# A streaming encoder layer on one core: convolution tiles in their own memory pool, two more gate tiles as half-size products, eight convolution blocks moved to the attention's end

## The chip, the cores and the metric

The kernel runs on one core of a Trainium2 chip. The metric is device microseconds (us) of one execution. Three timed runs of the kernel before gave a median of 1925.06 us (1923.37 to 1925.43). One more execution was taken with the hardware profiler, and every time of an instruction below comes from that one.

## The reference

One layer of an encoder, for 1024 new frames of one stream and 32 frames of a running one (1056 columns in all), model width 1024:

```
h = rmsnorm(x) * (1 + sc1) + sh1            # scale and shift from the conditioning
q, k, v, g, a, cb, cc, ch, ga, gb = split(h @ w_in)
S, o = gated_linear_attention(q, k, v, log_sigmoid(a @ w_alpha + b) / 16, S0)
o    = rmsnorm_per_head(o) * silu(g)
y_a  = o @ w_gla_out
conv = causal_conv3(cc * ch) ;  y_b = (cb * conv) @ w_conv_out
x    = x + g1 * ((sigmoid(ga) * y_a + sigmoid(gb) * y_b) @ w_o)
x    = x + g2 * (silu(h2 @ w_gate) * (h2 @ w_up)) @ w_ffn_out     # h2 = second norm of x
```

All is float32. The kernel writes each fp32 product as three fp32r products, of a high and a low part of each operand (high by high, low by high, high by low).

## The kernel before, in words

Work runs in stages, each bounded mostly by TensorE (PE): projections for the attention up to about 285 us of the profiled execution; attention with the convolution branch, about 285 to 658 us; the gate tiles g, ga, gb (24 tiles of 128 output rows, eight each), about 658 to 924 us; then the output projections and the feed-forward part. Activations `h` lie in SBUF as eight tiles of 128 rows, each as a high and a low part (names `h_558`, `h_559` and so on).

*Attention and convolution.* The prompt is handled in four pairs of chunks of 128 frames (`prompt()`). A pair runs through seven levels of products with masks (PE writes `pslv`, VectorE copies it under a mask into the scores `s_sb`, and VectorE builds the next level's operand `tt`), then the diagonal (PE `psdg`, VectorE L832 into `s_sb`). Then for each chunk come the transposes of k (PE `pst`), the output (PE `pso`, which reads `s_sb`), its norm (PE `pms`) and the state update (PE `psn`, VectorE L589); the last thing is the normalized output `oT` (VectorE L620). The convolution `conv()` is a generator of 72 blocks, nine for each of eight tiles: three projections (cc, ch, cb) by three column blocks (384, 384 and 288 columns), 24 matmuls a block (helper `mm`, L135, output `ps`). Each `yield` of the attention lets the driver put such blocks into PE's program. The results of a block are taken out of PSUM by ScalarE (cc) or VectorE (ch by cc, L878; cb by the convolved row, L897); GpSimd starts the convolution (L885) and VectorE ends it with two long operations (L889). What blocks the attention has not used up follow it. The tiles `ccs`, `u` and `acc` of the convolution lie in the same pool as the attention's (`gl`, L537).

*The gate tiles.* A full-size tile is a projection in the same form as a conv projection: 3 blocks, 72 matmuls. The others go in pairs of tiles (`h_pair`) by a seven-product scheme of half-size matrices, which needs 168 matmuls of 264 columns for two tiles. Its operands are sums and differences of the quarters of `h` (`h_sums`, called for k = 0 to 3): for each k VectorE makes four sums (L965), GpSimd four differences (L971), ScalarE casts four high parts (L976) and VectorE subtracts four low parts (L977). The products are called B11 and B21, which read `h` itself, and T1 to T4, which need those sums; PE's line for them is L1055, output `psH`. Weight sums (L999) become a high part on ScalarE (L942) and a low part on VectorE or GpSimd (L943). Before, the first two tiles of gb (j = 0 and 4) are full-size, and `h_sums` runs beside them; the other 22 tiles go in eleven pairs.

The results of `h_sums` lie in pool `r2`, which takes the memory of `gl` after it closes. The order in which instructions stand on each engine is fixed when the program is built.

Of the kernel before, what the change touches and what calls it, by code (L numbers as in the profile page):

```python
# [7 lines left out]
F32 = mybir.dt.float32  # L8
# [5 lines left out]
P = 128  # L14
# [54 lines left out]
def hybrid_trunk(  # L69
# [464 lines left out]
    g2c = [mods[:, s, 40:48] for s in range(2)]  # L534


    with tc.tile_pool(name="gl", bufs=1) as gl:  # L537

        ones_r = gl.tile([P, P], F32R, name="ones_r")
        nc.vector.tensor_copy(ones_r, ones)  # L540
# [262 lines left out]
        def prompt():  # L803
            state = None
            npair = S // 256
            pair = load_pair(0)
            Tt = prep_level(pair, 0)
            for pr in range(npair):
                Z0, Z1, BB, vs = pair
                SS = s_sb[pr % SSETS]  # L810
                for li in range(len(LEVELS)):
                    nxt = prep_level(pair, li + 1) if li + 1 < len(LEVELS) else None
                    if li == DGL:
                        diag = [prep_diag(pair, ab) for ab in range(2)]
                    yield 1
                    if li in (0, 3):
                        yield 1
                    ps = psx.tile([P, 512], F32, tag="x", name=nm("pslv"))
                    for hd in range(H):
                        mm(ps[:, hd * P : (hd + 1) * P], Tt[:, 0, hd, :], Tt[:, 1, hd, :], True, True)  # L820
                    for ab in range(2):
                        nc.vector.copy_predicated(
                            SS[ab], mview(2 * li + ab, H), ps.rearrange("p (h n) -> p h n", h=H)
                        )
                    Tt = nxt
                chunk = [prep_chunk(pair, ab, pr > 0 or ab > 0) for ab in range(2)]
                yield 1
                for ab in range(2):
                    ps = psx.tile([P, 512], F32, tag="x", name=nm("psdg"))
                    mm(ps, ones_r, diag[ab][0], True, False)  # L830
                    mm(ps, ones_r, diag[ab][1], False, True)
                    nc.vector.copy_predicated(  # L832
                        SS[ab], mview(2 * len(LEVELS), H), ps.rearrange("p (h n) -> p h n", h=H)
                    )
                if pr + 1 < npair:
                    pair = load_pair(pr + 1)
                for ab in range(2):
                    qs, ks, dec = chunk[ab]
                    yield 1
                    yield 1  # L840
                    kt, vsp = transpose_k(ks), split_v(vs[ab])
                    psos, sq = out_chunk(vs[ab], SS[ab], qs, state)
                    if ab == 1 and pr + 1 < npair:
                        Tt = prep_level(pair, 0)
                    yield 1
                    finish_chunk(psos, sq, 256 * pr + ab * P)
                    state = state_update(state, dec, kt, vsp)
            nc.scalar.dma_start(sp_out.rearrange("h p v -> p h v"), state)
# [17 lines left out]

        def conv():
            for j in range(KT):
                ccs = gt([P, T], "ccs", 2)
                u = gt([P, UE], "u", 2)  # L870
                acc = gt([P, T + 2], "acc", 1)

                def ev_cc(b, ps, ccs=ccs):
                    nc.scalar.copy(ccs[:, blk(b)], ps)

                def ev_ch(b, ps, ccs=ccs, u=u):
                    for lo, hi, nat in csegs(b):
                        nc.vector.tensor_tensor(nat(u, 2), ps[:, lo - BO[b] : hi - BO[b]], ccs[:, lo:hi], op=ALU.mult)  # L878

                nc.gpsimd.memset(u[:, 0:2], 0.0)  # L880
                nc.sync.dma_start(u[:, S + 2 : S + 4], cache[j])
                yield from gemm_steps(load_w(w_in[CC0 + j]), h, ev_cc)
                yield from gemm_steps(load_w(w_in[CH0 + j]), h, ev_ch)
                n = T + 2
                nc.gpsimd.tensor_scalar(  # L885
                    acc[:, :n], u[:, 0:n], convp[:, 0, j : j + 1], convp[:, 3, j : j + 1], op0=ALU.mult, op1=ALU.add
                )
                for i in (1, 2):
                    nc.vector.scalar_tensor_tensor(  # L889
                        acc[:, :n], u[:, i : i + n], convp[:, i, j : j + 1], acc[:, :n], op0=ALU.mult, op1=ALU.add  # L890
                    )
                nc.gpsimd.tensor_copy(cco[:, 0, j, :], u[:, S : S + 2])
                nc.gpsimd.tensor_copy(cco[:, 1, j, :], u[:, UE - 2 : UE])

                def ev_cb(b, ps, acc=acc, j=j, ccs=ccs):
                    for lo, hi, nat in csegs(b):
                        nc.vector.tensor_tensor(ccs[:, lo:hi], ps[:, lo - BO[b] : hi - BO[b]], nat(acc, 0), op=ALU.mult)  # L897
                    if b == NB - 1:
                        nc.scalar.dma_start(c_d[j], ccs[:, :T])

                yield from gemm_steps(load_w(w_in[CB0 + j]), h, ev_cb)
# [15 lines left out]
        nc.scalar.dma_start(cc_out, cco.rearrange("p s j r -> p (s j r)"))  # L917


    r2 = ctx.enter_context(tc.tile_pool(name="r2", bufs=1))  # L920

    t4 = ctx.enter_context(tc.tile_pool(name="t4", bufs=1, reuse_waits="tile"))

# [6 lines left out]
    def unit(tag, shape, dt=F32R):  # L930
        if tag == "r1":
            return r1.tile(shape, dt, tag="r1", name=nm("u"))
        return r2.tile(shape, dt, tag=tag, name=nm("u"), bufs={"a": 12, "x": 8}[tag])

    gran = [0]

    def granule(src, lo_eng):
# [4 lines left out]
        nc.scalar.copy(hi, src)  # L942
        lo_eng.tensor_tensor(lo, src, f(hi), op=ALU.subtract)  # L943
        return hi, lo

    def gate_block(j, b, ps):
        sb = td()[:, : wd(b)]
        nc.scalar.activation(sb, ps[:, : wd(b)], AF.Sigmoid)  # L948
        nc.scalar.dma_start(sb_d[j][:, blk(b)], sb)

# [6 lines left out]
    def h_sums(k):  # L959
        raw = []  # L960
        for kk in (k, k + 4):
            hi, lo = h[kk]
            for e in range(2):
                t = td().rearrange("p (q n) -> p q n", q=2)
                nc.vector.tensor_tensor(t, f(quarters(hi)[e]), f(quarters(lo)[e]), op=ALU.add)  # L965
                raw.append(t)
        b11, b12, b21, b22 = raw

        def sub(x, y):
            t = td().rearrange("p (q n) -> p q n", q=2)  # L970
            nc.gpsimd.tensor_tensor(t, x, y, op=ALU.subtract)  # L971
            return t

        def keep(i, t):
            u = unit("x" if i == T4 else "a", [P, 2, 2, CW])
            nc.scalar.copy(u[:, 0], t)  # L976
            nc.vector.tensor_tensor(u[:, 1], t, f(u[:, 0]), op=ALU.subtract)  # L977
            hsum[i][k] = u

        t1 = sub(b12, b11)  # L980
        keep(T1, t1)
        t2 = sub(b22, t1)
        keep(T2, t2)
        keep(T3, sub(b22, b12))
        keep(T4, sub(b21, t2))
# [111 lines left out]

        return done


    ws = [load_w(w_in[GB0 + j]) for j in (0, 4)]
    for n, (j, w) in enumerate(zip((0, 4), ws)):
        h_sums(2 * n)
        h_sums(2 * n + 1)
        gemm(w, h, lambda b, ps, j=j: gate_block(j, b, ps))
    for j in range(4):
        h_pair(G0, j, AF.Silu, done_g)
    for j in range(4):
        h_pair(GA0, j, AF.Sigmoid, done_to(sa_d))
    for j in range(1, 4):  # L1110
        h_pair(GB0, j, AF.Sigmoid, done_to(sb_d))

    some_done(99)
# [16 lines left out]
    for j in range(KT):  # L1130
        w = load_w(w_gla_out[j])
        if j < 2:
            pool, tag = ((psm, "m"), (psx, "x"))[j]
            ps = [pool.tile([P, 512], F32, tag=tag, name=nm("ps"))[:, : wd(b)] for b in range(NB)]
            for k in range(KT):
                for b in range(NB):
                    ah, al = og[k]
                    mm(ps[b], w[0][:, k, :], ah[:, blk(b)], k == 0, False)
                    mm(ps[b], w[0][:, k, :], al[:, blk(b)], False, False)
                    mm(ps[b], w[1][:, k, :], ah[:, blk(b)], False, k == KT - 1)  # L1140
            for b in range(NB):
                attn_block(j, b, ps[b])
        else:
            gemm(w, og, lambda b, ps, j=j: attn_block(j, b, ps))
        pr = tuple(unit("a" if j < 4 else "x", [P, T]) for _ in range(2))
        for q in range(2):
            craw = td()
            nc.sync.dma_start(craw, c_d[j][:, cols(q)])
            split(craw, pr[0][:, cols(q)], pr[1][:, cols(q)], "act", "pool")
        cpair.append(pr)  # L1150
# [71 lines left out]
    def make_ops(q):  # L1222
        n = 0
        for i in (B11, B21, T2, T3, T1, B22, T4):
            ops[q][i] = []
            for _ in range(2):
# [1 line left out]
                if q == 0 and n < 12:  # L1228
                    t = r2.tile(sh, F32R, tag="a", name=nm("op"), bufs=12)
                elif q == 0 or n < 6:  # L1230
                    t = r2.tile(sh, F32R, tag="x", name=nm("op"), bufs=8)
                else:
                    t = r1.tile(sh, F32R, tag="r1", name=nm("op"))
                ops[q][i].append(t)
# [314 lines left out]
    x1 = [None] * KT  # L1549

    def load_x1(j):
        x1[j] = r2.tile([P, T], F32, tag="x", name=nm("x1"), bufs=8)
        load(x1[j], x1_d[j])

    turns = [(p, j) for p in range(len(PARTS)) for j in range(4)]
# [265 lines left out]
```

## Time and profile before

| | |
|---|---|
| median of three timed runs | 1925.06 us |
| the profiled execution, its own time | 1930.39 us |
| its span | 1928.6 us |
| PE busy | 1834.0 us (95%) |
| VectorE (DVE) busy | 1382.9 us (72%) |
| ScalarE (ACT) busy | 790.1 us (41%) |
| GpSimd (POOL) busy | 797.7 us (41%) |
| mean granted clock of PE | 0.978 |

A row of instructions gives a line of the code, an engine, an operation, the tile written and the tiles read; where an engine sat idle, what it waited for follows an arrow. Clock 1.00 is TensorE's upper level.

### The profile page before, as it was taken

Reading aid. Unit: us, or ns where it says so; the run is one execution under the profiler, and the core shown is the slowest. Engines: PE = TensorE matmul, PEld = TensorE weight load, DVE = VectorE, ACT = ScalarE, POOL = GpSimd, SP = SyncE. Lnnn points to the kernel's source line nnn. Section 1 sums busy time; section 2 is a strip of 40 time slices with the busy share of each in tenths; the row PEclk is TensorE's granted clock in tenths of the full one; section 3 lists DMA queues with packets and bytes.
Section 4 is the critical chain, followed back from the end, with each engine's and each line's share of the span. In section 5 each row is a group of like instructions: output and inputs, shape, how many; then the busy total and the mean of one; then the engine's idle time right before and its main releaser. Section 6 shows DMA issues by size and latency. Waiting matters only on the chain. (4 is left out here: it accounts for less than half of the span.)

```text
span 1928.6 us, 35501 instructions
## 1 busy us (share of the span) xinstructions
PE 1834.0 (95%) x13517; PEld 1809.4 (94%) x13517; DVE 1382.9 (72%) x2543; ACT 790.1 (41%) x1641; POOL 797.7 (41%) x649
## 2 busy tenths in 40 slices
PE   6799889999999979999999999899999999999997
PEld 5698888999999979999999999899999999999997
DVE  7999967775866777543114478789888888678865
ACT  5434344444342355544212256435444444222243
POOL 6753437574754452112442243122223222255474
PEclk9799999999999989999999999999999999999998
DMA  7587644323221226335854454213433434686522
GB/s 276 179 286 230 210 167 129 99 89 94 88 77 56 87 88 231 134 110 195 308 178 135 127 175 151 78 61 128 172 131 129 171 126 151 212 299 235 213 95 90
DMA packets 166269, 298.45 MB, mean 155 GB/s; under 512 B 20593, under 2 KB 81905, under 8 KB 166098
## 3 DMA queue, kind: packets, MB, share of 16 engines
q1 hardware_dynamic: 117170, 211.90, 33.6%
q10 hardware_dynamic: 48928, 84.27, 11.8%
q8 instruction: 106, 1.74, 0.4%
q14 instruction: 65, 0.53, 0.1%
HBM read 211.78 MB, written 84.33 MB: 154 GB/s over the span
## 5 line engine op out<-in xcount | busy, mean ns | idle before, releaser
L135 PE MATMUL ps<-h,whi 128*128 128x384 f32 (+2 forms) x1440 | 347.3, 326 | 6.9 <-DVE vst L518 4.8
L143 POOL TENSOR_TENSOR wlo<-raw,whi 128x512 fp32r<-128x512 f32 (+2 forms) x160 | 218.1, 1382 | 298.9 <-ACT whi L139 212.9
L1330 PE MATMUL psX<-op,wg 128*128 128x264 f32 (+1 forms) x2112 | 273.2, 286 | 6.3 <-DVE bz L1361 3.9
L1330 PEld LDWEIGHTS psX<-op,wg 128*128 128x128 f32 x2112 | 264.2, 189 | 9.1 <-DVE bz L1361 5.9
L135 PEld LDWEIGHTS ps<-h,whi 128*128 128x128 f32 x1440 | 251.8, 190 | 8.2 <-issue 5.2
L943 POOL TENSOR_TENSOR wg<-raw,wg 128x512 fp32r<-128x512 f32 x66 | 96.9, 1468 | 367.0 <-ACT wg L942 304.3
L135 PE MATMUL ps<-h,wlo 128*128 128x384 f32 (+2 forms) x720 | 233.6, 325 | 0.0
L135 PE MATMUL ps<-u,whi 128*128 128x264 f32 (+2 forms) x1064 | 226.2, 306 | 2.1 <-ACT whi L139 1.9
L135 PEld LDWEIGHTS ps<-u,whi 128*128 128x128 f32 x1064 | 176.3, 189 | 3.0 <-ACT whi L139 2.1
L135 PE MATMUL ps<-u,wlo 128*128 128x264 f32 (+2 forms) x532 | 162.8, 306 | 0.0
L224 DVE CUSTOM_DVE_ANT_0 junk<-wm,cb 128x1024 f32<-128x1024 f32 x96 | 153.7, 1601 | 4.9 <-DMA wm<-in_w_modT 3.4
L1330 PE MATMUL psV<-op,wg 128*128 128x264 f32 (+1 forms) x1056 | 137.9, 286 | 1.1 <-ACT wg L942 1.1
L135 PEld LDWEIGHTS ps<-h,wlo 128*128 128x128 f32 x720 | 136.8, 190 | 0.2 <-issue 0.2
L1055 PE MATMUL psH<-u,wg 128*128 128x264 f32 x1056 | 133.6, 286 | 3.2 <-ACT wg L942 3.2
L1055 PEld LDWEIGHTS psH<-u,wg 128*128 128x128 f32 x1056 | 131.1, 190 | 3.7 <-ACT wg L942 3.7
L1330 PEld LDWEIGHTS psV<-op,wg 128*128 128x128 f32 x1056 | 133.2, 189 | 1.3 <-ACT wg L942 1.3
L139 ACT CAST whi<-raw 128x512 fp32r<-128x512 f32 (+2 forms) x164 | 87.7, 579 | 103.5 <-PE ps L135 58.6
L942 ACT CAST wg<-d 128x512 fp32r<-128x512 f32 x132 | 81.6, 622 | 109.4 <-PE psV L1330 36.0
L943 DVE TENSOR_TENSOR wg<-d,wg 128x512 fp32r<-128x512 f32 x121 | 92.7, 768 | 44.2 <-ACT wg L942 43.9
L1055 PE MATMUL psH<-h,wg 128*128 128x264 f32 x792 | 101.9, 287 | 5.9 <-ACT d L948 5.9
L1611 PE MATMUL psX<-u,wg 128*128 128x264 f32 x768 | 106.2, 284 | 0.0
L1055 PEld LDWEIGHTS psH<-h,wg 128*128 128x128 f32 x792 | 99.3, 190 | 6.1 <-ACT d L948 6.1
(321 smaller groups left out, 4019.5 us busy)
## 6 DMA issues: line engine op xcount, KB each, us to landing
wm<-in_w_modT SPq DMA_DIRECT2D x64, 512.0 KB, 4.5
raw<-in_w_in SPq DMA_DIRECT2D x124, 256.0 KB, 3.2
op_d<-st ACTq DMA_DIRECT2D x56, 528.0 KB, 5.1
u<-op_d SPq DMA_DIRECT2D x56, 528.0 KB, 6.1
raw<-in_w_ffn_in SPq DMA_DIRECT2D x88, 256.0 KB, 3.2
u<-og_d SPq DMA_DIRECT2D x16, 528.0 KB, 8.4
raw<-in_w_o SPq DMA_DIRECT2D x32, 256.0 KB, 3.1
raw<-in_w_ffn_out SPq DMA_DIRECT2D x32, 256.0 KB, 5.1
```

Of the source, the lines that this page charges most:

```text
L135: nc.tensor.matmul(ps, lhsT, rhs, start=start, stop=stop)
L139: nc.scalar.copy(hi, raw)
L143: nc.gpsimd.tensor_tensor(lo, raw, f(hi), op=ALU.subtract)
L224: nc.vector.tensor_tensor_reduce(junk, wm, cb[:, st, :], 1.0, 0.0, ALU.mult, ALU.add, mods[:, st, j : j + 1])
L942: nc.scalar.copy(hi, src)
L943: lo_eng.tensor_tensor(lo, src, f(hi), op=ALU.subtract)
L1055: nc.tensor.matmul(bank[i][q], wt[l][:, k, :], h_operand(i, k, q, r), start=i in (B11, B21, T3) and k == 0 and n == 0, stop=k == 3 and n == 2,
L1330: nc.tensor.matmul(ps, l[:, k, :], r[:, k, :], start=first and k == 0 and i == 0, stop=k == 3 and i == 2, skip_group_check=True,)
L1611: nc.tensor.matmul(ps, w[l][:, k, :], o[k][:, r, c], start=first and k == 0 and i == 0, stop=k == n - 1 and i == 2, skip_group_check=True,)
```

## The change

1. A new pool `cv` is opened before `gl` and holds `ccs`, `u` and `acc` of the convolution. The pool `r2` is split: `r2x` (tag "x", five buffers) lies where `cv` was, `r2` (tags "a", twelve, and "y", three) where `gl` was, and both wait for the tiles whose memory they take, one by one, not for the whole pool. With this the `h_sums` need no longer follow the convolution's end.
2. One of two `yield 1` between the diagonal and the transposes of a chunk goes, eight in all.
3. The two full-size gate tiles go: gb's j = 0 and 4 become a twelfth pair, and the four `h_sums` stand ahead of all pairs.

```diff
-    with tc.tile_pool(name="gl", bufs=1) as gl:
+    with tc.tile_pool(name="cv", bufs=1) as cv, tc.tile_pool(name="gl", bufs=1) as gl:
...
                     qs, ks, dec = chunk[ab]
                     yield 1
-                    yield 1
                     kt, vsp = transpose_k(ks), split_v(vs[ab])
...
-                ccs = gt([P, T], "ccs", 2)
-                u = gt([P, UE], "u", 2)
-                acc = gt([P, T + 2], "acc", 1)
+                ccs = cv.tile([P, T], F32, tag="ccs", name=nm("ccs"), bufs=2)
+                u = cv.tile([P, UE], F32, tag="u", name=nm("u"), bufs=2)
+                acc = cv.tile([P, T + 2], F32, tag="acc", name=nm("acc"), bufs=1)
...
-    r2 = ctx.enter_context(tc.tile_pool(name="r2", bufs=1))
+    r2x = ctx.enter_context(tc.tile_pool(name="r2x", bufs=1, reuse_waits="tile"))
+    r2 = ctx.enter_context(tc.tile_pool(name="r2", bufs=1, reuse_waits="tile"))
...
-    ws = [load_w(w_in[GB0 + j]) for j in (0, 4)]
-    for n, (j, w) in enumerate(zip((0, 4), ws)):
-        h_sums(2 * n)
-        h_sums(2 * n + 1)
-        gemm(w, h, lambda b, ps, j=j: gate_block(j, b, ps))
+    for k in range(4):
+        h_sums(k)
     for j in range(4):
         h_pair(G0, j, AF.Silu, done_g)
     for j in range(4):
         h_pair(GA0, j, AF.Sigmoid, done_to(sa_d))
-    for j in range(1, 4):
+    for j in range(4):
         h_pair(GB0, j, AF.Sigmoid, done_to(sb_d))
```

The rest of the diff gives later users of the old eight "x" buffers one of "x" or "y" each.

On PE the program is the same up to the last row of the block after `psdg` of pair 0. There, before, a second block of 24 matmuls stood ahead of the transposes:

```order
L135 MATMUL ps_3491<-h_608,wlo_3380 128x288
L135 MATMUL ps_3534<-h_558,whi_3524 128x384
...
L135 MATMUL ps_3534<-h_608,wlo_3525 128x384
L560 MATMUL pst_3562<-ident,kk_3425 128x128 x4
L135 MATMUL pso_3575<-s_sb_2735,v_3009 128x128 x4
L135 MATMUL pso_3580<-s_sb_2735,v_3009 128x128 x4
```

Now the transposes stand right behind the first block, and two matmuls of the next block ahead of `pso`:

```order
L135 MATMUL ps_3494<-h_608,wlo_3383 128x288
L560 MATMUL pst_3522<-ident,kk_3428 128x128 x4
L135 MATMUL ps_3569<-h_558,whi_3559 128x384
L135 MATMUL ps_3569<-h_559,whi_3559 128x384
L135 MATMUL pso_3535<-s_sb_2738,v_3012 128x128 x4
L135 MATMUL pso_3540<-s_sb_2738,v_3012 128x128 x4
```

So 24 conv matmuls left this place; in each of the four pairs there are now 24 between `psdg` and the first transposes, and were 48. Within the first three steps between levels the conv matmuls of pair 1 go from 24, 24, 48 to 27, 13, 38, of pair 2 from 21, 18, 48 to 7, 28, 36 (its last four steps from 24 each to 8, 22, 21 and 22, and 17 instead of 4 ahead of its first level), of pair 3 from 26, 19, 48 to 24, 27, 23.

The second place is PE behind the attention. Before, the last norm product `pms` was followed by the rest of three conv blocks (70 conv matmuls), three blocks of the first full-size gate tile (from `ps_6507`), one of the second, and then the first half-size products:

```order
L135 MATMUL pms_6246<-nrm_6214,ones_r 128x512
...
L135 MATMUL ps_6507<-h_558,whi_6431 128x384
...
L135 MATMUL ps_6647<-h_558,whi_6441 128x384
...
L1055 MATMUL psH_6743<-h_588,wg_6776 128x264
```

Now the same `pms` is followed by the last three projections of the convolution (first rows `ps_6138`, `ps_6226`, `ps_6325`) and then by half-size products at once:

```order
L135 MATMUL pms_5990<-nrm_5958,ones_r 128x512
...
L135 MATMUL ps_6138<-h_558,whi_6128 128x384
...
L135 MATMUL ps_6226<-h_558,whi_6216 128x384
...
L135 MATMUL ps_6325<-h_558,whi_6315 128x384
...
L1052 MATMUL psH_6558<-h_558,wg_6566 128x264
L1052 MATMUL psH_6559<-h_558,wg_6566 128x264
```

Behind `pms` there are now 242 conv matmuls, 172 more than before, and no full-size gate tile. The products B11 and B21 (48 matmuls) stand before T3 and T2 in both programs. The second PSUM bank of B11 (`psH_6559`) is the one that conv block `ps_6325` leaves.

The third place is VectorE at the attention's end. Before, the last convolution results (L897) and a weight's low part stood between the last `oT` and the first sums:

```order
L620 SCALAR_TENSOR_TENSOR oT_6245<-pso_6199,glag,nrm_6250 128x4x128
L897 TENSOR_TENSOR ccs_5973<-ps_6350,acc_5975 128x128 x3
L897 TENSOR_TENSOR ccs_5973<-ps_6378,acc_5975 128x128 x2
L897 TENSOR_TENSOR ccs_5973<-ps_6378,acc_5975 128x32
L943 TENSOR_TENSOR wg_6747<-raw_6731,wg_6747 128x512
L965 TENSOR_TENSOR d_6451<-h_558,h_559 128x528
L965 TENSOR_TENSOR d_6453<-h_558,h_559 128x528
```

Now the sums (L962, which was L965) follow `oT` directly, and the last conv tile's operations stand among them:

```order
L620 SCALAR_TENSOR_TENSOR oT_5989<-pso_5943,glag,nrm_5994 128x4x128
L962 TENSOR_TENSOR d_6438<-h_558,h_559 128x528
...
L945 TENSOR_TENSOR wg_6566<-raw_6550,wg_6566 128x512
...
L877 TENSOR_TENSOR u_6124<-ps_6226,ccs_6123 128x128 x3
...
L888 SCALAR_TENSOR_TENSOR acc_6125<-u_6124,convp,acc_6125 128x1058
...
L896 TENSOR_TENSOR ccs_6123<-ps_6325,acc_6125 128x128 x3
...
L945 TENSOR_TENSOR wg_6630<-d_6628,wg_6630 128x512
```

Among the 32 rows of the sums there are now nine small rows of L877, nine of L896, two long ones of L888 and one L945; GpSimd has its conv operation (L884) and one weight part among its sixteen differences. The low part of T2's first weights (`wg_6630`) stands at the end of the sums in both programs.

## Rows read from the trace of the kernel before

**Rows 1.** The page: busy time, share of the span and instructions.

```profile
PE 1834.0 (95%) x13517; PEld 1809.4 (94%) x13517; DVE 1382.9 (72%) x2543; ACT 790.1 (41%) x1641; POOL 797.7 (41%) x649
```

**Rows 2.** Stretches (us): length, busy by engine (instructions), granted clock, DMA share, GB/s.

```profile
657.82:669.38 11.56, 11.56 (x74) 11.56 (x73) 9.54 (x11) 3.21 (x6) 7.91 (x5) 1.00 0.54 172
720.00:900.00 180.00, 180.00 (x1484) 180.00 (x1483) 100.09 (x168) 91.67 (x204) 40.07 (x28) 1.00 0.46 154
645.80:657.82 12.02, 12.02 (x77) 11.97 (x77) 10.46 (x19) 3.60 (x4) 3.37 (x5) 1.00 0.28 92
657.82:702.36 44.54, 33.34 (x199) 32.40 (x197) 40.62 (x43) 17.70 (x32) 28.06 (x18) 0.88 0.22 72
690.00:695.00 5.00, 0.00 (x0) 0.00 (x0) 4.87 (x6) 1.37 (x3) 3.65 (x3) 0.66 0.00 0
396.50:652.00 255.50, 247.66 (x1644) 244.35 (x1643) 179.08 (x285) 99.89 (x178) 145.72 (x117) 0.99 0.25 78
```

**Rows 3.** Waits of PE, 655 to 710: waiting for, us in total, times, longest.

```profile
PE psH L1055 <- ACT d L948: 5.9, 1, 5.9
PE psH L1055 <- ACT wg L942: 3.2, 2, 2.4
PE ps L135 <- ACT d L948: 2.1, 1, 2.1
```

**Rows 4.** Timeline of VectorE: start us, duration us, instruction, idle before.

```profile
655.20 1.41 DVE L620 SCALAR_TENSOR_TENSOR oT<-pso,glag,nrm 128x512 f32<-128x512 f32 x2
660.41 1.93 DVE L965 TENSOR_TENSOR d<-h,h 128x528 f32<-128x528 f32 x3
698.79 0.69 DVE L977 TENSOR_TENSOR u<-d,u 128x528 fp32r<-128x528 f32 x1
701.89 1.28 DVE L943 TENSOR_TENSOR wg<-d,wg 128x512 fp32r<-128x512 f32 x2
```

**Rows 5.** Groups by line, 660.3 to 699.6: busy us, mean ns, idle before.

```profile
L971 POOL TENSOR_TENSOR d<-d,d 128x528 f32<-128x528 f32 x16 | 26.3, 1662 | 11.5 <-DVE d L965 8.3 <-DMA sb_d<-d 3.1
L977 DVE TENSOR_TENSOR u<-d,u 128x528 fp32r<-128x528 f32 x16 | 22.5, 1415 | 1.9 <-ACT u L976 1.3
L965 DVE TENSOR_TENSOR d<-h,h 128x528 f32<-128x528 f32 x16 | 13.7, 898 | 1.3 <-POOL d L971 1.2
```

**Rows 6.** Timeline of VectorE, operations of the convolution.

```profile
656.53 0.68 DVE L897 TENSOR_TENSOR ccs<-ps,acc 128x128 f32<-128x128 f32 x3
647.83 2.46 DVE L889 SCALAR_TENSOR_TENSOR acc<-u,convp,acc 128x1058 f32<-128x1058 f32 x1 [0.88 <-POOL acc L885]
650.81 1.31 DVE L889 SCALAR_TENSOR_TENSOR acc<-u,convp,acc 128x1058 f32<-128x1058 f32 x1
```

**Rows 7.** Timeline of PE: first output products of each pair, and the last norm product.

```profile
363.36 0.39 PE L135 MATMUL pso<-s_sb,v 128*128 128x128 f32 x2
447.24 0.39 PE L135 MATMUL pso<-s_sb,v 128*128 128x128 f32 x2
531.55 0.39 PE L135 MATMUL pso<-s_sb,v 128*128 128x128 f32 x2
615.39 0.28 PE L135 MATMUL pso<-s_sb,v 128*128 128x128 f32 x1
645.80 0.40 PE L135 MATMUL pms<-nrm,ones_r 128*128 128x512 f32 x1
```

**Rows 8.** Timeline of VectorE: the diagonals into the scores, pairs 0 to 3; then pair 1's last level.

```profile
361.16 1.36 DVE L832 COPY_PREDICATED s_sb<-masks,psdg 128x512 f32<-128x512 uint8 x2
441.21 1.35 DVE L832 COPY_PREDICATED s_sb<-masks,psdg 128x512 f32<-128x512 uint8 x2
526.63 1.36 DVE L832 COPY_PREDICATED s_sb<-masks,psdg 128x512 f32<-128x512 uint8 x2
607.45 1.35 DVE L832 COPY_PREDICATED s_sb<-masks,psdg 128x512 f32<-128x512 uint8 x2
435.06 0.75 DVE L751 TENSOR_TENSOR tt<-tt,z 128x512 f32<-128x512 f32 x1 [2.62 <-DMA z<-q_d]
```

More of the change, by code (lines that the diff above doesn't have):

```diff
@@ L932, in unit @@
             return r1.tile(shape, dt, tag="r1", name=nm("u"))
-        return r2.tile(shape, dt, tag=tag, name=nm("u"), bufs={"a": 12, "x": 8}[tag])
+        if tag in ("x", "y"):
+            return (r2x if tag == "x" else r2).tile(shape, dt, tag=tag, name=nm("u"), bufs={"x": 5, "y": 3}[tag])
+        return r2.tile(shape, dt, tag=tag, name=nm("u"), bufs=12)
     gran = [0]
@@ L944, in granule @@
         return hi, lo
[L946 to L949, printed above, removed]
     B11, B21, B22, T4, T1, T2, T3 = range(7)
@@ L974, in keep @@
         def keep(i, t):
-            u = unit("x" if i == T4 else "a", [P, 2, 2, CW])
+            u = unit("a" if i != T4 else "y" if k < 3 else "x", [P, 2, 2, CW])
             nc.scalar.copy(u[:, 0], t)
@@ L1144, in hybrid_trunk @@
             gemm(w, og, lambda b, ps, j=j: attn_block(j, b, ps))
-        pr = tuple(unit("a" if j < 4 else "x", [P, T]) for _ in range(2))
+        pr = tuple(unit("a" if j < 4 else "y" if 2 * j + r > 12 else "x", [P, T]) for r in range(2))
         for q in range(2):
@@ L1230, in make_ops @@
                 elif q == 0 or n < 6:
-                    t = r2.tile(sh, F32R, tag="x", name=nm("op"), bufs=8)
+                    t = unit("y" if n in (0, 1, 2) else "x", sh)
                 else:
@@ L1551, in load_x1 @@
     def load_x1(j):
-        x1[j] = r2.tile([P, T], F32, tag="x", name=nm("x1"), bufs=8)
+        x1[j] = unit("y" if j < 3 else "x", [P, T], F32)
         load(x1[j], x1_d[j])
```

## The prediction

> **What bounds the kernel now.** I read the page's busy shares first: PE is busy 95% of the span, VectorE 72% [rows 1]. So PE's program is the length of the kernel, except where PE stands still or runs at the low clock. Then the stretches around the change, one after the other. In 720 to 900 us PE has no gap at the granted clock 1.00 and does 1484 half-size matmuls in 180.00 us, 0.1213 us each [rows 2]: here only the number of matmuls counts. In the attention, 396.5 to 652, PE is busy 247.66 of 255.50 us and VectorE 179.08, 70% [rows 2]: PE leads, because conv blocks fill its waits. Between them, from 657.82 to 702.36, PE is busy 33.34 of 44.54 us at a mean clock of 0.88 [rows 2]. That is the one soft place. The waits of PE there add up to 11.2 us: 5.9 and 2.1 behind ScalarE, 3.2 for a weight's high part [rows 3]. In 690 to 695 PE does nothing, and VectorE is busy 4.87 of 5 us [rows 2]. So VectorE's sums set this place, and from 660.41, their start, to 702.36, when the low part of T2's first weight exists (701.89, two operations of 1.28 us in all), 41.95 us pass [rows 4].
>
> **Part 1, two gate tiles.** A full-size tile takes 11.56 us at clock 1.00 [rows 2]; two are 23.12 us. The twelfth pair takes 168 half-size matmuls at 0.1213 us, 20.38 us. Difference: -2.74 us, sure, as both run where PE leads. The weights of a pair cost ScalarE and VectorE more than those of two full tiles, but VectorE is busy 100.09 and ScalarE 91.67 of the 180 us [rows 2], and PE never waits there, so this is hidden.
>
> **Part 2, the hand-over.** Measure it from the last `pms` (645.80 [rows 7]) to the start of T2. Before that is 56.56 us (702.36 less 645.80). PE's work in it: 12.02 us of attention and conv [rows 2], 23.12 us of full tiles, 48 products of B11 and B21 at 0.1213, 5.82; in all 40.96. Lost: 15.6 us, of which 11.2 are waits and the rest low clock.
>
> Now PE's work there is 12.02 us, plus 172 conv matmuls, plus the same 5.82. A conv matmul costs the 72nd part of a tile, so 172 are 27.6 us: 45.44 in all. VectorE sets the length again, if the sums do not become quicker. They start directly behind `oT`, whose end is 656.61 (655.20 and 1.41), 10.81 us behind `pms`; before it was 14.61. Then they take 41.95 us, and what the last conv tile puts among them. Eighteen small operations in six groups of three at 0.68 us are 4.1 us; two long ones lie between 1.31 and 2.46 us each, so 2.6 to 4.9 [rows 6]; one weight part is 0.64 (half of the two at 701.89 [rows 4]) or, beside GpSimd, some twice that. That is 7.3 to 10.3 us on VectorE. It has under 4 us of idle in the sums [rows 5], which can swallow some. GpSimd gets a conv operation and a weight part too, and each of its differences already holds up VectorE. Bounds: 5 us (idle swallowed) and 11; I take 8, near the sum of the rows with a little swallowed. T2 then starts 10.81 + 41.95 + 8 = 60.8 us behind `pms`, and 60.8 less 45.4 gives 15.3 us lost: -0.3 us against before, with bounds of -3.3 and +2.7.
>
> PE cannot use this time with something else. B11's second bank is left by conv block `ps_6325`, which VectorE takes out late in the sums, some twelve operations before T2's weight; PE is in order, so T3 and T2 stand behind it. The conv tail moved here fills PE, but PE had full-size tiles here before: one cover replaces the other.
>
> Why the sums are slow matters here. L977 alone took 0.69 us (at 698.79, after GpSimd's last difference [rows 4]); beside GpSimd's differences its mean was 1415 ns [rows 5]. The Trainium skill, "SBUF — State Buffer", section "Who interferes with whom", says that a VectorE instruction with two SBUF inputs contends with a GpSimd instruction that reads SBUF, and that one with at most one SBUF input does not. The rows agree with the first half. By the second half the eighteen small conv operations, which read one input from PSUM, would leave GpSimd free to run, and then only the two long ones and the conv operation on GpSimd would lengthen the sums, about 5 us; the sum by that reading is the lower bound of this part.
>
> **Part 3, the attention's cover.** The same 172 matmuls, 27.6 us, leave the attention. Where PE is the bound there, this time is gone from it, and part 2 has counted it at the other end. What comes back as waiting is the cost. The place is `pso`, which needs `s_sb` with the diagonal. 24 conv matmuls ahead of it are 4.2 us (two blocks of a tile are 384 columns and one is 288; 24 of 384 take 4.2 of the 11.56 us).
>
> - Pair 0: `pso` came at 363.36 [rows 7], would come at 359.5 (4.2 less, two conv matmuls put ahead); the scores are complete at 362.52 (361.16 and 1.36 [rows 8]), the first chunk's at about 361.8. Wait 2.3 to 3.0, I take 2.7.
> - Pair 1: 447.24 less 4.2 is 443.0, scores at 442.56: no wait from this alone. But 18 conv matmuls (2.9 us at 11.56/72 each) also left the steps between the first levels, while VectorE's chain waits 2.62 us for a load at 435.06 [rows 8] and will not come earlier for it. Wait 0 to 2.5, I take 2.2.
> - Pair 2: 531.55 less 4.2 is 527.35, scores at 527.99: 0.6. Between its levels 39 are fewer (6.3 us), against 13 more ahead of the first (2.1 us); if nothing of VectorE's chain moves up, 6.9, and with the 13 as cover 4.8. I take 2.0, nearer to the place's own 0.6, as VectorE's idle 30% [rows 2] lets part of its chain move up.
> - Pair 3: 615.39 less 4.2 is 611.2, scores at 608.80: room of 2.4; 19 fewer between levels (3.1 us) leave 0 to 0.7. I take 0.5.
>
> Together 7.4 us, with bounds of 0 (pair 0 waits, and other waits shrink by as much) and 13.1, or more if the levels themselves begin to wait. VectorE has one conv tile less to do in the attention, which helps it; that is why I do not add to the sum for the levels.
>
> **Part 4, the rest.** The new pool, the buffer tags and the later loads change which tile waits for which. The stages behind run without PE waits of size, and the order there is nearly the same; 0.
>
> **The sum.** -2.7, -0.3 and +7.4 give +4.4 us. The profiled execution took 1930.39 us, so it would take 1934.8. The median is 5.3 us lower, so the forecast on its scale is 1929.5 us.
>
> **The rivals.**
>
> A. Faster: the attention has slack. VectorE is idle 30% of it and gets less to do, so behind pair 0 its chain moves up with PE, and what pair 0 waits comes back from waits between levels that shrink; and the sums take only 5 us more (the reading of part 2). Then -2.7, -3.3 and 0: -6.0, 1919 us. For it: VectorE's 70%. Against it: its idle time there is waiting for loads and for PE's own levels, as at 435.06, which a shorter PE program does not move up. It would be still less if the sums hid wholly behind the conv tail, but 41.95 us of sums do not fit beside the 28.8 us of it that are left behind `oT` (12.02 and 27.6 less 10.81).
>
> B. No change: the waits in the attention are about 3 us, hand-over as forecast: 1925 us. This differs from the forecast only in the size of part 3.
>
> C. Much slower: sums and conv lock each other, and the levels wait too. VectorE and GpSimd run almost in turn in the sums; if every conv operation also delays a GpSimd difference on which a later L977 waits, part 2 becomes +2.7, and if the six steps between levels that lost ten conv matmuls or more wait 1 us more each, part 3 becomes 7.4 and 6 and, with pair 2 at 4.8, 16.2: 1941 us. It decides from the point where VectorE's chain between levels is longer than the conv left there, as with the 7 matmuls (1.1 us) in pair 2.
>
> D. The change does not do what it says: the sums still wait for the attention's memory. A unit may not be written before the tiles under it are free, and `oT` is among them until it is stored. For it: the sums are the first users of that memory. Against it: VectorE's first sums are not in that pool. If so the sums start as late as before, 3.8 us later than I reckon: +8.2, 1933 us.
>
> **Chances.** Forecast (slower by 2 to 7 us) 0.40, A 0.27, B 0.18, C 0.07, D 0.08. A measurement of this kernel can tell about 0.2%, 3.85 us, from no change. Faster by more than that is most of A: 0.23. Slower by more is the upper half of the forecast, C and D: 0.42. Within: 0.35. The range must hold A and reaches towards C: 1918 to 1937. The forecast's own is 1927 to 1932.
>
> **What would show it.** Right: a wait of PE for L832 of 2 to 3 us before `pso` in pair 0 and shorter ones in pairs 1 and 2; a gap of PE of over 10 us after the last conv block, ended by the eviction of `ps_6325` or by VectorE; T2 about 61 us behind the last `pms`; 0.1213 us for a half-size matmul as before. Wrong: no new wait at `pso` (then A), T2 earlier than 57 us behind `pms` (the sums got quicker), or a changed length of the stages behind 924 us, which I hold at nothing.

## The result and the profile after

Five timed runs of the changed kernel have a median of 1939.23 us (1935.28 to 1939.77), those of the kernel before 1925.06. The ratio is 1.0061, 95% interval 1.005 to 1.0072: the change costs about 12 us, as the ratio has it, or 14 by the medians. The forecast was +4.4, and its range ended at 1937: 0.2 us above the time that the ratio gives (1936.8), and below the median.

The first trace of the changed kernel looks like the forecast. Its execution took 1935.28 us, the fastest of the five, and 4.9 us more than the profiled one of before, which was slower than every timed run shown with it. Busy shares, to set against [rows 1]:

```profile
PE 1831.7 (95%) x13541; PEld 1807.8 (94%) x13541; DVE 1393.5 (72%) x2557; ACT 791.8 (41%) x1651; POOL 800.9 (41%) x648
```

PE has 2.3 us less to do, as two full-size tiles less one pair promised (2.7), and VectorE 10.6 more. Waits of PE from 300 to 720 us, against [rows 3]: what, us in total, times, longest.

```profile
PE pslv L135 <- DVE tt L752: 9.2, 5, 4.4
PE psH L1052 <- DVE ccs L896: 8.2, 1, 8.2
PE pso L135 <- DVE s_sb L832: 4.1, 3, 2.2
PE psH L1052 <- ACT wg L944: 3.0, 1, 3.0
PE pss L135 <- DVE tts L661: 2.3, 1, 2.3
PE pslv L135 <- DVE state L589: 1.9, 1, 1.9
```

In the kernel before, the largest group of waits in the attention was the one at the levels, and L832 was not among them:

```profile
PE pslv L135 <- DVE tt L752: 6.5, 6, 2.0
```

The waits at `pso` for L832 are new, and so is the one for B11's second bank (L896). The largest new one of the attention is 4.4 us at a level. The timeline of PE shows where they stand (start, duration, instruction, idle before), against [rows 7]:

```profile
359.85 2.05 PE L135 MATMUL pso<-s_sb,v 128*128 128x128 f32 x16 [2.24 <-DVE s_sb L832]
405.31 1.18 PE L135 MATMUL pslv<-tt 128*128 128x128 f32 x8 [4.35 <-DVE tt L752]
626.39 0.40 PE L135 MATMUL pms<-nrm,ones_r 128*128 128x512 f32 x1
665.86 1.62 PE L1052 MATMUL psH<-h,wg 128*128 128x264 f32 x12
675.64 6.29 PE L1052 MATMUL psH<-h,wg 128*128 128x264 f32 x36 [8.16 <-DVE ccs L896]
684.89 10.89 PE L1052 MATMUL psH<-u,wg 128*128 128x264 f32 x72 [2.96 <-ACT wg L944]
```

The last norm product came 19.4 us earlier. But 2.1 us of that is an earlier start: pair 0's diagonal, ahead of which every engine has the same instructions in both kernels, stands at 352.56 us here and at 354.61 in the trace of before. From the diagonal on, the attention is 17.4 us shorter, so 10.2 of the 27.6 us of moved cover came back. The first products of the sums start 58.5 us behind the last norm product. And VectorE's conv operations among the sums, against [rows 6]:

```profile
654.78 0.67 DVE L877 TENSOR_TENSOR u<-ps,ccs 128x128 f32<-128x128 f32 x3
664.78 2.52 DVE L888 SCALAR_TENSOR_TENSOR acc<-u,convp,acc 128x1058 f32<-128x1058 f32 x1 [1.06 <-POOL acc L884]
668.94 2.38 DVE L888 SCALAR_TENSOR_TENSOR acc<-u,convp,acc 128x1058 f32<-128x1058 f32 x1
```

But this pair of traces explains 4.9 us (6.9 from the diagonal on: 1580.9 against 1574.0), not 12 to 14. Two more traces close the gap. Stretches of a second execution of before (`before_2`, span 1923.9 us; columns as in [rows 2]): attention from pair 0's diagonal to the last norm product, of it the part up to pair 1's diagonal, then to T2, then to the gate tiles' end.

```profile
351.17:640.79 289.62, 281.85 (x1886) 277.76 (x1885) 201.25 (x326) 116.27 (x205) 165.49 (x133) 1.00 0.26 80
351.17:434.08 82.91, 79.61 (x529) 77.96 (x529) 62.88 (x99) 35.17 (x63) 54.46 (x45) 1.00 0.31 94
640.79:697.35 56.56, 45.36 (x274) 44.36 (x273) 51.11 (x62) 21.26 (x36) 31.42 (x23) 0.91 0.24 77
697.35:911.38 214.03, 214.03 (x1749) 214.03 (x1750) 113.99 (x192) 108.68 (x240) 49.57 (x36) 0.99 0.48 165
```

The same of a third execution of the changed kernel (`after_3`, span 1936.5 us), whose diagonal began as early, at 349.89:

```profile
349.89:627.14 277.25, 260.83 (x1711) 256.12 (x1711) 201.32 (x310) 113.00 (x196) 160.64 (x128) 0.98 0.25 78
349.89:432.81 82.92, 76.08 (x482) 74.67 (x481) 64.73 (x99) 34.53 (x61) 52.09 (x44) 0.94 0.28 85
627.14:685.62 58.48, 47.06 (x300) 46.63 (x299) 51.46 (x74) 17.53 (x30) 34.10 (x23) 0.94 0.20 65
685.62:921.67 236.05, 236.01 (x1921) 235.78 (x1922) 124.30 (x209) 118.91 (x263) 54.29 (x39) 0.99 0.46 159
```

Here the attention is only 12.4 us shorter (289.62 less 277.25), so 15.2 of the 27.6 us came back. The spans differ by 12.6: start -1.3, attention -12.4, hand-over +1.9, gate tiles behind it +22.0 (236.05 less 214.03), stages behind +2.3. This is the size that the timed runs have.

### The profile page after: what moved, and what is told of

Same layout as the page of the kernel before. It is cut to its first block, busy times and chain, and to the rows that moved or that the text cites. A ratio compares the mean times of both kernels' runs of the same rounds, so it can differ in the third digit from the quotient of the medians.

```text
span 1933.5 us, 35576 instructions
## 1 busy us (share of the span) xinstructions
PE 1831.7 (95%) x13541; PEld 1807.8 (94%) x13541; DVE 1393.5 (72%) x2557; ACT 791.8 (41%) x1651; POOL 800.9 (41%) x648
## 3 DMA queue, kind: packets, MB, share of 16 engines
q10 hardware_dynamic: 48640, 84.27, 11.8%
## 4 chain that ended last, share of the span: by engine, by line
PE 49%; DVE 9%; issue 2%; ACT 2%; DMA 2%; POOL 0%; ACTq 0%; DVEq 0%; SPq 0%; POOLq 0%
PE ps L135 13%; PE psH L1052 12%; PE psX L1323 9%; PE psX L1604 5%; PE psV L1323 4%; PE psV L1604 2%; PE psW L1323 2%; DVE st L1454 1%; PE psW L1604 1%; DVE wg L945 1%; DVE op L1233 1%; DVE au L1357 1%; DVE au L1369 1%; DMA u<-x_d 1%; DVE e L1195 1%
## 5 line engine op out<-in xcount | busy, mean ns | idle before, releaser
L135 PE MATMUL ps<-h,whi 128*128 128x384 f32 (+2 forms) x1344 | 328.5, 329 | 4.8 <-DVE vst L518 4.8
L945 POOL TENSOR_TENSOR wg<-raw,wg 128x512 fp32r<-128x512 f32 x68 | 99.4, 1462 | 370.8 <-ACT wg L944 332.4
L135 PEld LDWEIGHTS ps<-h,whi 128*128 128x128 f32 x1344 | 238.9, 193 | 5.7 <-issue 5.1
L135 PE MATMUL ps<-h,wlo 128*128 128x384 f32 (+2 forms) x672 | 220.3, 328 | 0.0
L1323 PE MATMUL psX<-op,wg 128*128 128x266 f32 (+1 forms) x1584 | 207.6, 287 | 7.0 <-DVE bz L1354 4.5
L1323 PEld LDWEIGHTS psX<-op,wg 128*128 128x128 f32 x1584 | 199.3, 189 | 9.5 <-DVE bz L1354 6.4
L1052 PE MATMUL psH<-u,wg 128*128 128x264 f32 x1152 | 146.3, 287 | 3.0 <-ACT wg L944 3.0
L1052 PEld LDWEIGHTS psH<-u,wg 128*128 128x128 f32 x1152 | 143.8, 190 | 3.4 <-ACT wg L944 3.2
L945 DVE TENSOR_TENSOR wg<-d,wg 128x512 fp32r<-128x512 f32 x124 | 95.9, 775 | 49.1 <-ACT wg L944 48.9
L1052 PE MATMUL psH<-h,wg 128*128 128x264 f32 x864 | 111.2, 288 | 8.2 <-DVE ccs L896 8.2
L1323 PE MATMUL psV<-op,wg 128*128 128x264 f32 (+1 forms) x792 | 104.7, 285 | 1.0 <-ACT wg L944 1.0
L135 PE MATMUL psv<-vhi,h 128*128 128x256 f32 x512 | 97.1, 288 | 6.3 <-ACT vst L516 5.0
```

Of the source, the lines that this page charges most:

```text
L135: nc.tensor.matmul(ps, lhsT, rhs, start=start, stop=stop)
L1052: nc.tensor.matmul(bank[i][q], wt[l][:, k, :], h_operand(i, k, q, r), start=i in (B11, B21, T3) and k == 0 and n == 0, stop=k == 3 and n == 2,
L1323: nc.tensor.matmul(ps, l[:, k, :], r[:, k, :], start=first and k == 0 and i == 0, stop=k == 3 and i == 2, skip_group_check=True,)
```

## The experiments

Each is timed in turn with the kernel before on one chip; medians of before lay between 1925.5 and 1926.0.

**1. The changed kernel again.**

> The changed kernel once more, for a second profile and a second interval. Its first profiled execution was 4.9 us longer than that of the kernel before (1935.3 against 1930.4), while the medians differ by 14.2 (1939.2 against 1925.1). Theory: the change costs what the two traces show, 4.9 us at the gate tiles' end (cover lost in the attention 27.6 less 19.4, hand-over +1.9, gate tiles 22.3 against 20.4), and the rest is what executions of one program differ by; then a second pair of profile and runs gives a ratio near 1.003. Rival: there is a further loss of 7 to 9 us that the first profiled execution happened not to have; then the ratio is again about 1.006, and this profile, if it is one near 1939, shows the loss in one place.

Measured: 1938.41 us, ratio 1.0058 (1.0045 to 1.0071). By the timed runs the rival holds: the loss is there again. The profile did not show it: it was one of the faster executions again (1936.69), with its diagonal late, at 354.56.

**2 and 3. Single executions of both, for their traces.**

> The kernel before once more, for a second trace. In its first profiled execution the diagonal of pair 0 began at 354.61 us, in five others of kernels with the same program up to there at 350.06 to 354.56. Theory: executions differ by up to 5 us ahead of that point, and the first trace of before was a late one; from the diagonal of pair 0 to the end it is 1574.0 us again within 1 us, and the whole execution is nearer to 1926. Rival: the stretch behind that point varies by 3 us or more.

> The changed kernel a third time, for its trace. From the diagonal of pair 0 to the end it took 1580.9 and 1580.3 us. Theory: again 1580 to 1582, and the execution's time follows from when that diagonal begins (352 to 358 us). Rival: the stretch behind varies, and a median near 1938.5 comes from there.

Measured: before 1925.68 us, the changed kernel 1938.24. For before the theory nearly held: a start earlier by 3.4 us came through to the end (1572.7 us from the diagonal on, 1574.0 in the first trace). For the changed kernel the rival held: 1586.6 us from the diagonal on, not 1580 to 1582. Its last norm product stands at 626.39, 628.29 and 627.14 us for diagonals at 352.56, 354.56 and 349.89, so the early start was lost, 3.4 us of it inside the attention. The stretch from pair 0's diagonal to pair 1's took 80.31, 81.01 and 82.92 us. What differs there is told under part 3 below.

**4. The pools alone.**

The new pools `cv`, `r2x` and `r2` as in the change; both yields and the two full-size tiles as before. Against the changed kernel, as are the other cuts unless said otherwise:

```diff
                     yield 1
+                    yield 1
...
-    for k in range(4):
-        h_sums(k)
+    ws = [load_w(w_in[GB0 + j]) for j in (0, 4)]
+    for n, (j, w) in enumerate(zip((0, 4), ws)):
+        h_sums(2 * n)
+        h_sums(2 * n + 1)
+        gemm(w, h, lambda b, ps, j=j: gate_block(j, b, ps))
...
-    for j in range(4):
+    for j in range(1, 4):
         h_pair(GB0, j, AF.Sigmoid, done_to(sb_d))
```

> The kernel before with the pools of the changed kernel alone: convolution tiles in their own pool, r2 split, both yields and both full-size gate tiles as before. Theory (the pools by themselves cost and gain next to nothing, VectorE sets the sums): within 3 us of the kernel before, 1923 to 1928. Rival (the 6 us between the medians that the traces' hand-over does not show come with the pools): 1930 to 1933.

Measured: 1924.89 us, ratio 0.9997 (0.9988 to 1.0005). The pools cost nothing.

**5. The cover back in the attention.**

```diff
                     yield 1
+                    yield 1
                     kt, vsp = transpose_k(ks), split_v(vs[ab])
```

> The changed kernel with the second yield back, so that the conv blocks cover the attention as before, and no full-size gate tile. Theory (attention loses nothing, and VectorE's sums set T2's start whatever PE has to do): from pair 0's diagonal to the last norm product 290 to 291 us as before; T2 53 to 57 us behind it, with only 17.8 us of PE work in there; then 168 more half-size products, 20.4 us: 17 to 20 us more than the kernel before, 1942 to 1946, so 4 to 7 more than the changed kernel. Rival (the lost cover of the attention is the whole loss, the hand-over adapts): 7 to 10 us less than the changed kernel, about 1930.

Measured: 1945.74 us, ratio 1.0099 (1.0084 to 1.0115). Attention 289.2 us, the first products of the sums 53.5 us behind it, though PE waits 35.2 us there: close to the theory's 290 to 291 and 53 to 57. The rival is out. Moving the conv blocks was right once the full-size tiles were gone; it gave back 7 us. Taking the tiles out was the costly part: the pools alone took 1924.89 us, the pools and a twelfth pair in place of the two tiles 1945.74.

**6. Thinning the cover in two pairs only.** The second yield back `if pr in (0, 2)`, and in the counterpart `if pr in (1, 3)`.

> The changed kernel with the second yield back in pairs 0 and 2 alone (the cover is thinned in pairs 1 and 3 only; 125 conv matmuls behind the last state product, were 220). Against the early trace of before, the pairs of the changed kernel's third trace got shorter by 0.0, 7.1, 1.1 and 4.2 us for 7.7, 8.0, 7.7 and 5.0 us of conv taken out. Theory (the loss sits in pairs 0 and 2, whose VectorE chains run into the next pair's first levels): the last norm product stands at 630 to 631 us, T2 about 58 us behind it; 1940 to 1942. Rival (the loss is spread by the number of conv matmuls taken out): last norm product at 635, 1945 to 1947.

> The counterpart: second yield back in pairs 1 and 3, cover thinned in pairs 0 and 2 only (150 conv matmuls behind the last state product). Theory: nearly all of the 16 us taken out of pairs 0 and 2 comes back as waits and low clock, the last norm product at 638 to 639, T2 58 us behind it; 1948 to 1951. Rival (spread evenly): 633 to 634, 1943 to 1945.

Measured: 1942.09 us (ratio 1.0085, 1.0071 to 1.0099) and 1945.61 (1.011, 1.0094 to 1.0125). From diagonal 0 to the last norm product 283.1 and 285.7 us, against 289.6. So thinning pairs 1 and 3 gave 6.5 of 12.4 us (77 conv matmuls), and thinning pairs 0 and 2 gave 3.9 of 16.4 (102). Pairs 0 and 2 are the worse ones, as the theory said, but the others are not free: 76% came back in the one and 48% in the other. The first kernel's median and last norm product (631.8) lie at the theory's end. The second's last norm product (638.1) is the theory's, but its median lies between the two expectations. The two traces also show what the cover in pair 0 does for the second level of pair 1. The first row has it (second yield back in pair 0), the second has not:

```profile
402.81 1.13 PE L135 MATMUL pslv<-tt 128*128 128x128 f32 x8 [1.28 <-DVE tt L752]
406.74 2.05 PE L135 MATMUL pslv<-tt 128*128 128x128 f32 x8 [4.33 <-DVE tt L752]
```

**7. The differences of the sums on VectorE.**

```diff
-            nc.gpsimd.tensor_tensor(t, x, y, op=ALU.subtract)
+            nc.vector.tensor_tensor(t, x, y, op=ALU.subtract)
```

> The changed kernel with the sixteen differences of the sums on VectorE instead of GpSimd. Theory (VectorE and GpSimd hold each other up there: 0.65 us alone, 1.3 to 2.4 beside one another): 48 operations at 0.65 are 31 us, with conv and weight parts about 41 in place of the 50 from the first sum to the last; T2 starts 7 to 9 us earlier, about 50 us behind the last norm product; 7 to 9 us less than the changed kernel, about 1931. Rival (VectorE is slow there by its number of operations): sixteen more at about 1.3 us, T2 10 to 20 us later, about 1950 to 1960.

> The kernel before with the same sixteen differences on VectorE. Theory: the 42 us from the first sum to T2's weight become about 33, the idle time of PE of 11.2 us mostly goes: 8 to 11 us less than the kernel before, about 1916. Rival (number of operations): 5 to 15 us more, about 1935.

Measured: 1930.44 us (ratio to before 1.0019, 1.0011 to 1.0028), 8 us less than the changed kernel; and 1918.40 (0.9954, 0.9941 to 0.9966), faster than both. In the changed kernel the first products of the sums moved from 58.5 to 51.8 us behind the last norm product. Groups of the sums in the kernel before with the differences moved, against [rows 5]:

```profile
L977 DVE TENSOR_TENSOR u<-d,u 128x528 fp32r<-128x528 f32 x16 | 11.0, 699 | 0.0
L971 DVE TENSOR_TENSOR d<-d,d 128x528 f32<-128x528 f32 x16 | 10.9, 702 | 1.6 <-DMA sb_d<-d 1.5
L965 DVE TENSOR_TENSOR d<-h,h 128x528 f32<-128x528 f32 x16 | 10.6, 697 | 0.0
```

All 48 operations now take 0.70 us each, 32.5 in all, less than the 36.2 that the 32 took beside GpSimd's 26.3 [rows 5]. That VectorE, reading two SBUF inputs, is held up there by GpSimd's differences is shown; the number of operations is not what bounds. Whether GpSimd is held up as well, no run shows.

**8. The full-size tiles as cover, with the new pools.** The two tiles behind the convolution's end, eleven pairs; then with the second yield in pairs 0 and 2; then with the differences on VectorE as well.

```diff
     for k in range(4):
         h_sums(k)
+    for j in (0, 4):
+        gemm(load_w(w_in[GB0 + j]), h, lambda b, ps, j=j: gate_block(j, b, ps))
...
-    for j in range(4):
+    for j in range(1, 4):
         h_pair(GB0, j, AF.Sigmoid, done_to(sb_d))
```

> The changed kernel with the two full-size gate tiles back, now as 144 matmuls between the convolution's last block and the first half-size products (eleven pairs). Theory (VectorE's sums set T2's start, 58.5 us behind the last norm product, and PE has only 45.4 us of work until then): PE now has 12.0 + 27.6 + 23.1 + 5.8 = 68.5 us, so nothing waits; gate stage shorter by 20.4 and T2 10 us later, and no low clock behind a gap: 10 to 12 us less than the changed kernel, about 1928. Rival (the loss sits in the attention or in the stages behind, and the gap does not matter): the two tiles only cost their 2.7 us, 3 us more than the changed kernel, about 1942.

> The kernel with the new pools, the two full-size gate tiles kept as cover behind the convolution, and the cover thinned in pairs 1 and 3 only. Theory: last norm product at about 630.5 against 640.8 before; PE has 12.0 + 12.4 + 23.1 + 5.8 = 53 us of work until T2, VectorE's sums want about 58, so T2 at about 688 against 697.4: 7 to 10 us less than before, 1915 to 1919. Rival (the waits in the attention grow with any thinning): no better than before, 1924 or more.

> The same, with the sixteen differences on VectorE. Theory: the sums want about 50 us and PE's 53 us decide, T2 at about 684: 12 to 15 us less than before, 1910 to 1914, so faster than the kernel before with the differences moved alone (1918.4). Rival (PE waits elsewhere in the hand-over, as for the PSUM bank that ScalarE or VectorE leaves late): 1917 to 1920.

Measured: 1930.34 us (1.0019, 1.0009 to 1.0029), 1931.95 (1.0034, 1.0021 to 1.0046) and 1926.55 (1.0, 0.9991 to 1.0009). The first is 8 us less than the changed kernel: PE's work counts in the hand-over, but 10 to 12 was expected; PE still waited 5.9 us for L896. The second missed its theory; its time lies in the rival's range, but not by the rival's mechanism, for its attention took 284.4 us, 5 less than before. The third missed both ranges, though the wait that its rival named is the one that came. What was overlooked is in the trace of the second: PE's one long wait in the hand-over, and ScalarE's timeline before it.

```profile
PE ps L135 <- ACT d L952: 11.8, 1, 11.8
```

```profile
688.23 0.63 ACT L979 CAST u<-d 128x528 fp32r<-128x528 f32 x1 [2.37 <-POOL d L974]
691.18 0.63 ACT L979 CAST u<-d 128x528 fp32r<-128x528 f32 x1 [2.32 <-POOL d L974]
691.83 1.28 ACT L952 ACT_TABLE_LOAD   x1
693.12 0.49 ACT L952 ACTIVATE d<-ps 128x384 f32<-128x384 f32 x1
```

The first eviction of a full-size block (the sigmoid, L952) stands in ScalarE's queue behind the casts of the sums, which wait for GpSimd's differences (25.8 us of waiting from 640 to 710). So its bank of PSUM, the memory that PE writes to, stays full, and PE waits for it. In the third kernel the same wait is still 6.6 us. The kernel before shows it too, 5.9 us for `d` L948 [rows 3], named in the prediction but not read so. No run moves these evictions, so how much of the miss they make is not shown.

## Why the prediction was right or wrong

The direction was right, and the waits came to about what was reckoned; what a wait costs beyond itself was priced at nothing, and so the sum, +4.4, is short by 7 to 10 us. The time lies outside the forecast's own 1927 to 1932. That it lies inside 1918 to 1937 by the ratio is luck: the upper end was set to reach towards rival C. By the steps:

**Part 1 (-2.7)** holds: 1478 half-size matmuls in the 180.00 us from 720 to 900, as many as before within missing records, no waits among them.

**Part 2 (-0.3)**: VectorE sets the hand-over, with the gap that ends at L896. First products of the sums at 58.5 us, forecast 60.8. Lost time 58.5 less 45.4 is 13.1 us, against 15.6: -2.5, inside the bounds. Of the two readings of the sums, 58.5 us is near the lower one (10.81, 41.95 and 5 make 57.8). Behind it the gate tiles took 22.0 us more, not 20.4. That is mostly a matter of where the count starts: in the kernel before, four products of the sums ran ahead of the short gap that ends where T2 was counted from.

```profile
695.79 0.76 PE L1055 MATMUL psH<-u,wg 128*128 128x264 f32 x4 [2.37 <-ACT wg L942]
697.35 4.72 PE L1055 MATMUL psH<-u,wg 128*128 128x264 f32 x24 [0.81 <-ACT wg L942]
```

Counted in both kernels from the first product that reads the sums, the hand-over went from 55.0 us (`before_2`) to 58.5 (`after_3`), and the gate tiles from 215.6 to 236.05, 20.5 more, as reckoned. The low clock is not what differs: over the first 14.38 us from T2 the granted clock is 0.88 in both.

```profile
697.35:711.73 14.38, 14.38 (x105) 14.38 (x106) 7.18 (x12) 6.67 (x15) 4.32 (x3) 0.88 0.34 102
685.62:700.00 14.38, 14.34 (x103) 14.11 (x104) 8.03 (x14) 7.67 (x17) 4.23 (x3) 0.88 0.34 103
```

By this count 14.0 us were lost before (55.0 less 41.0) and 13.1 now; by the other, -2.5 and 1.6. Either way part 2 comes to -0.9, near enough.

**Part 3 (+7.4, bounds 0 to 13.1)** is the step that fell short: 15.2 us in the pair of early traces, outside the bounds. It has two pieces. Waits: those of `after_3` behind its first diagonal add up to 16.4 us, those of `before_2` to 7.7; the difference of 8.7 is near the 7.4 reckoned, but the places differ, so that the sum fits is luck (2.3 at pair 0, for 2.7; 1.3 at pair 2, for 2.0; nothing at pair 1's `pso`, but 4.3 at its second level, for which nothing was taken). The other 6.5 us is slower work: PE's busy time fell by 21.0 us (281.85 less 260.83) and not by 27.6. That was priced at nothing. The rows of `after_3` around the wait at the level:

```profile
404.27 2.05 PE L135 MATMUL pslv<-tt 128*128 128x128 f32 x8 [4.33 <-DVE tt L752]
```

```profile
400.00:405.00 5.00, 0.73 (x3) 0.76 (x4) 5.00 (x5) 0.94 (x2) 5.00 (x4) 0.79 0.06 16
405.00:410.00 5.00, 5.00 (x20) 5.00 (x19) 5.00 (x8) 1.70 (x4) 4.03 (x4) 0.53 0.68 196
```

PE is busy 0.73 of 5 us, and in the next 5 us it is fully busy at a granted clock of 0.53, near the 1.2 GHz level; in `before_2` the clock is 1.00 in both stretches, with waits of 1.5 and 1.2 us at the same two levels. A wait of 4.3 us so costs more than itself.

How much comes back differs from one execution to the next, and five traces show one reason. The kernels of `e_subD_after` (experiment 7) and `e_gate` (the first of experiment 8) have the changed kernel's attention, with the same instructions in the same order on every engine up to the last norm product. Against `before_2`, with 289.62 us, PE busy for 281.85 and at a clock of 1.00:

| trace | pair 0's diagonal | attention | PE busy | came back | of it waits | of it slower work | clock, 5 us from pair 0's `pso` |
|---|---|---|---|---|---|---|---|
| `after` | 352.56 | 273.83 | 259.38 | 11.8 | 6.7 | 5.1 | 1.00 |
| `after_again` | 354.56 | 273.73 | 258.65 | 11.7 | 7.3 | 4.4 | 1.00 |
| `e_subD_after` | 353.15 | 274.88 | 258.76 | 12.9 | 8.4 | 4.5 | 1.00 |
| `e_gate` | 350.06 | 276.93 | 260.63 | 14.9 | 8.5 | 6.4 | 0.66 |
| `after_3` | 349.89 | 277.25 | 260.83 | 15.2 | 8.7 | 6.5 | 0.66 |

The wait of 4.3 to 4.4 us at pair 1's second level is in all five, with the low clock behind it. The wait of 2.2 to 2.3 us for L832 at pair 0's `pso` is in all five too, but only in the two early ones the clock fell behind it:

```profile
359.85:364.85 5.00, 5.00 (x34) 5.00 (x35) 3.83 (x7) 1.83 (x4) 3.65 (x5) 1.00 0.50 136
357.20:362.20 5.00, 4.96 (x25) 4.97 (x26) 3.26 (x7) 1.82 (x3) 3.68 (x5) 0.66 0.44 138
```

The first row is `after`, the second `after_3`. So part 3 measures 11.7 to 15.2 us, of which waits are 6.7 to 8.7. The first pair of traces showed 10.2 because the first execution of before had a slow stretch of its own: behind a wait of 2.05 us at a level the clock fell, which it did not in `before_2` behind 2.03 us, and its attention took 291.2 us.

Why VectorE is late at that level: ahead of it stand the norm of pair 0's second chunk and pair 1's first level in one queue, without a gap:

```profile
398.09 1.36 DVE L822 COPY_PREDICATED s_sb<-masks,pslv 128x512 f32<-128x512 uint8 x2
399.35 1.61 DVE L751 TENSOR_TENSOR tt<-tt,z 128x512 f32<-128x512 f32 x1
400.88 1.57 DVE L618 TENSOR_TENSOR nrm<-nrm,nrm 128x512 f32<-128x512 f32 x1
402.38 1.75 DVE L752 TENSOR_TENSOR tt<-tt,z 128x512 f32<-128x512 f32 x1
```

VectorE's 70% was read as room (part 3 took nothing for the levels). At a change of pairs it is full, and the conv blocks that went had covered just that: with those of pair 0 back, the wait is 1.28 us again (experiment 6).

**Part 4 (0)** holds for the pools (experiment 4). The 2.3 us behind the gate tiles in `after_3` are not in the two other traces of the changed kernel (1012.4 and 1012.0 us from the output projection to the end, 1012.4 and 1012.5 before); one execution, cause open.

**The rivals.** A is out: its hand-over was nearly right, but what pair 0 waits did not come back from the levels, whose waits grew. B's 3 us is out. C comes nearest in size (1941 us), with a chance of 0.07; it named waits at the levels, but six of 1 us more, where one of 3 us more came, without the clock, and with a longer hand-over that did not come. D is out: the sums start directly behind `oT`, at 636.51. What the prediction took from the Trainium skill, "SBUF — State Buffer", section "Who interferes with whom", agrees with experiment 7 in its first half (1415 ns beside GpSimd, 699 without it). Its second half, that operations with at most one SBUF input do not contend, fits the small PSUM-fed ones, 0.57 to 0.68 us for three in the sums; T2 came 2.3 us earlier than the sum taken.

**The scale.** The sum was set on one profiled execution of before, lying 5.3 us above the median, and taken down by that. That is sound only if a late start is all that sets one execution apart from another. Before passes a late start on nearly in full; in the changed kernel the two early executions lost 2.0 to 3.5 us in the attention against the three later ones, 1.7 to 2.6 of it ahead of pair 1's diagonal, where the clock fell behind the wait at `pso`. Two of five traces show this; why its timed executions mostly lie higher than its first two profiled ones is not settled beyond that, nor why the clock fell behind that wait in the one case and not in the other.

## What to carry to other kernels

Filler in a PE-bound stage is to be priced where it stands: not by the other engine's mean busy share, but by its queue at the place, and a wait that appears costs also the slow clock behind it (here 6.7 to 8.7 us of waits and 4.4 to 6.5 of slower work). When the engine that sets a hand-over runs beside one that holds it up, take that one out of it before moving cover around: one word changed gave 7.5 us, all of the reshuffling lost 12. Compare two traces of each kernel before trusting a difference of 5 us.

## What the runs showed of the hardware that was not expected

- A difference on VectorE took 0.70 us. On GpSimd it took 1.66 us, and VectorE's subtractions of low parts beside it 1.42 in place of 0.70. With sixteen operations more on the busier engine the first products of the sums came 6 to 7 us earlier.
- The same instruction (pair 0's diagonal), with the same order on every engine up to there, was reached between 348.7 and 354.6 us by the executions of all these kernels, and between 349.9 and 354.6 by those of the changed kernel alone.
- The granted clock fell to 0.53 for 5 us behind a wait of 4.3 us, and stayed at 1.00 in the same place behind waits of 1.5 and 1.2 us. Behind a wait of 2.2 to 2.3 us at one instruction it fell in two executions (0.66 over 5 us) and not in three others.
